# Output projection in two groups of 1024 columns, with the weight sums of the first group formed in DRAM

## Chip, cores and metric

One core of a Trainium2 chip runs the whole kernel. The metric is the device time of one execution in microseconds. All times are of this one core: the median of the runs of the kernel before, and the span of one profiled execution.

## What is computed

One layer of a bidirectional encoder: an RMS norm, one input projection, attention with eight heads over 512 tokens, a recurrent group (convolution and two linear scans), gates, and an output projection that is added to the input. The change touches the last of these alone. Cut to what matters:

```python
def hybrid_layer(x, norm_w, w_in, ..., w_out):
    h = rms_norm(x, norm_w)
    proj = jnp.einsum('bsd,de->bse', h, w_in)
    ...
    mixed = jnp.concatenate([rms_norm(attn_out, attn_norm_w) * jax.nn.silu(g_attn),
                             rms_norm(lru_out, lru_norm_w) * jax.nn.silu(g_lru)], axis=-1)
    return x + jnp.einsum('bse,ed->bsd', mixed, w_out)
```

`x` has 512 rows and 2048 columns, `mixed` 512 by 2048, `w_out` 2048 by 2048, all float32.

## The kernel before

**Numbers.** Each float32 operand of a matmul is split into a rounded high part (a cast on ScalarE, ACT) and the rest (a subtraction on VectorE, DVE). A product is then three matmuls: high by high, high by low, low by high. A weight block therefore costs a DMA, a cast and a subtraction before TensorE (PE) can use it.

**Order.** PE's instructions stand in the order in which the code is written. ACT, DVE, GpSimd (POOL) and SyncE (SP, which issues nearly all DMAs) are ordered by a scheduler that takes ready instructions by priority; loads and splits of weights get a high one. In every engine an instruction that waits holds up all behind it.

**Start.** The first input projection multiplies the first 512 columns of the recurrent input while x arrives: SP loads x in eight chunks (`xload`, L221) beside the weights (`wraw`, L191), PE transposes them (L228), DVE forms sums of squares (L237). `xstats` makes of these `rstd`: a sum on DVE (L270), then two small operations on POOL (`rsqrt_mean`, L254 and L255). `rows` turns `rstd` into a broadcast row `rbc`: four products with the identity on DVE (L263), one matmul on PE (L265), one copy. Every result of a projection is multiplied by `rbc` when it leaves PSUM (`evac_bc`, L364). The splits of the projections' weights are L202 (ACT) and L203 (DVE).

**Middle.** The other projections fill PE while the recurrences and the attention run. POOL computes small norms and scales the softmax weights (L566).

**Output stage.** `outputs` (L704) works in four groups of 512 columns. The 16 row blocks of `w_out` are taken in eight pairs of 256 rows; `mixed` is kept as eight pairs of features in the same way. For the first six pairs a group uses the seven-product form of a 2 by 2 block product (four sums of weight blocks, L670 to L672, and four sums of feature blocks made once, `build`), each product 256 tokens by 256 columns, that is two row tiles of three matmuls with 256 columns (L727). The last two pairs use the plain eight products with 512 columns (L748). The four products that several results share (P1, Q6, Q5, Q7) have PSUM banks of their own and are combined on DVE after the sixth pair (L780 to L787); the others and the plain ones accumulate in the results' banks. At a group's end the residual `xt` is added (L793) and stored through SP (L794). In the last group one row tile is split into two halves of 256 columns so that the last add and store are small.

Of the kernel before, what the change touches and what calls it, by code (L numbers as in the profile page):

```python
# [16 lines left out]
P = 128  # L17
# [38 lines left out]
def hybrid_kernel(  # L56
# [45 lines left out]
    ps = ctx.enter_context(tc.tile_pool(name="ps", bufs=4, space=bass.MemoryType.PSUM))  # L102

# [583 lines left out]
    def four(src, hi, lo):  # L687
        src = halves(src)
        nc.scalar.copy(hi, src)
        nc.vector.tensor_sub(lo, src, f(hi))  # L690

# [3 lines left out]
    def wkept(n):  # L695
        i = turn_of[0] % 3
        turn_of[0] += 1
        pool = pools["out" if i else "fin"]
        return [
            pool.tile([P, 7, H], F32R, tag=f"{t}{i}", bufs=1, name=nm(t))[:, :n]  # L700
            for t in ("wh", "wl")
        ]

    def outputs(work):  # L704

        for c in range(DM // SEQ):
            xt, comb = (
                pools["out"].tile([P, NT, SEQ], F32, tag=t, bufs=1, name=nm(t)) for t in ("xt", "cb")
            )
            cs = slice(c * SEQ, (c + 1) * SEQ)  # L710
            rows_ = [slice(t * P, (t + 1) * P) for t in range(NT)]
            for t in range(NT):
                nc.sync.dma_start(xt[:, t], xf[rows_[t], cs])

            acc = {k: pj().rearrange("p (s e) -> p s e", e=H) for k in (P1, Q6, Q5, Q7)}
            own = [mm() for _ in range(NT)]
            fresh = set(acc) | set(range(NT))

            def mult(k, s, ah, al, a, bh, bl, b_, last):
                ts_ = slice(s * P, (s + 1) * P)  # L720
                if k in acc:
                    dst, bank = acc[k][:, s, :], k
                else:
                    bank = s if k == Q4 else 2 + s
                    dst = own[bank][:, H:] if k in (P2, Q4) else own[bank][:, :H]
                for lh, rh in ((ah, bh), (ah, bl), (al, bh)):
                    nc.tensor.matmul(  # L727
                        dst, lh[:, a, ts_], rh[:, b_, :], start=bank in fresh,
                        stop=last and s == 1 and rh is bh and lh is al, skip_group_check=True,
                    )  # L730
                    fresh.discard(bank)


            end = c == DM // SEQ - 1
            lasts = [pj()[:, :H], own[1][:, H:]] if end else []

            def whole(t, ah, al, bh, bl, last):

                ts_ = slice(t % 2 * P, (t % 2 + 1) * P)
                for half in range(2 if t == 1 and end else 1):  # L740
                    for k in range(2):
                        a, w = 2 * k + t // 2, slice(2 * k, 2 * k + 2)
                        dst = own[t].rearrange("p (j e) -> p j e", e=H)
                        if t == 1 and end:
                            dst, w = lasts[half], 2 * k + half
                        for j, (lh, rh) in enumerate(((ah, bh), (ah, bl), (al, bh))):
                            new = t == 1 and end and half == 0 and k == 0 and j == 0 and not last
                            nc.tensor.matmul(  # L748
                                dst, lh[:, a, ts_], rh[:, w], start=new,
                                stop=last and k == 1 and j == 2, skip_group_check=True,  # L750
                            )

            for i, (r0, A) in enumerate(mixed):
                with tc.high_priority(AHEAD):
                    (raw,) = wraw(w_out, r0, c * SEQ)
                    if i < 6:
                        bh, bl = wkept(7)
                        seven(raw, ALU.add, bh, bl)
                    else:
                        bh, bl = wkept(4)  # L760
                        four(raw, bh, bl)
                if c == 0:
                    next(work, None)
                    A = mixed[i][1]
                ah, al = A
                if i < 6:
                    for k in (P1, Q6, Q5, Q7, P2, Q3, Q4):
                        for s in range(2):
                            mult(k, s, ah, al, k[0], bh, bl, k[1], i == 5 and k in (P1, Q6, Q5, Q7))
                else:  # L770
                    for t in (2, 3, 0, 1):
                        whole(t, ah, al, bh, bl, i == 7)
                if i == 5:
                    with tc.high_priority(AHEAD):

                        def blk(i, j):
                            return comb[:, 2 * i : 2 * i + 2, j * H : (j + 1) * H]

                        v2 = fin_s((P, 2, H))
                        nc.scalar.copy(blk(1, 1), acc[P1])  # L780
                        nc.vector.tensor_sub(v2, acc[Q6], blk(1, 1))
                        nc.vector.tensor_add(blk(1, 0), acc[Q5], v2)
                        nc.vector.tensor_add(blk(0, 0), acc[Q7], blk(1, 0))
                        nc.vector.scalar_tensor_tensor(
                            blk(0, 1), acc[Q7], -1.0, v2, op0=ALU.mult, op1=ALU.subtract
                        )
                        nc.vector.tensor_add(xt, xt, comb)  # L787
            with tc.high_priority(AHEAD):
                parts = [(t, 0, SEQ, own[t]) for t in (2, 3, 0, 1)]
                if end:  # L790
                    parts[3:] = [(1, j * H, (j + 1) * H, lasts[j]) for j in range(2)]
                for t, e0, e1, src in parts:
                    nc.vector.tensor_add(xt[:, t, e0:e1], src, xt[:, t, e0:e1])  # L793
                    nc.sync.dma_start(  # L794
                        of[rows_[t], cs.start + e0 : cs.start + e1], xt[:, t, e0:e1]
                    )
# [60 lines left out]
    lru_consts()  # L857
    fill = proj_feat(C_XR + SEQ, a2)
# [4 lines left out]

    def kv_proj():
        yield from proj_tok(C_K, a3)
# [12 lines left out]
    def q_proj(c0, acc):  # L878
        yield from proj_tok(c0, acc)
        rots.append(norm_rope(evac_tok(acc, ev), G, rq))  # L880
# [15 lines left out]
    def gates():  # L896
        todo = iter(())
        for n, (c0, row) in enumerate(((C_GL, R_LN), (C_GL + SEQ, R_LN + 4), (C_GA, R_AN))):
            acc, wait = [], 0
            for k, _ in enumerate(proj_feat(c0, acc)):  # L900
                if n == 0 and k >= 16 and k % 4 == 0:
# [116 lines left out]
```

## Time and profile before

| | us |
|---|---|
| median of three runs (668.01 to 669.76) | 669.5 |
| span of the profiled execution (first to last instruction) | 668.2 |
| output stage, first to end of last matmul | 500.83 to 664.54 |
| PE busy / DVE busy / ACT busy / POOL busy | 662.1 / 486.2 / 331.5 / 56.8 |
| mean granted TensorE clock | 1.000 |

The page gives the busy time of each engine, the chain of work that ended last, and the costliest groups of instructions with their mean duration. An engine that is busy nearly all the time and makes up the chain sets the time. "Busy" of PE counts overlapping matmuls, so the pace of matmuls is the distance between their starts. DMA shares are of the 16 DMA engines.

The DMA busy share over the span, in 40 slices of 16.7 us, and what was moved:

```profile
DMA  8843252322244311421122211232335364362711
GB/s 286 273 138 95 64 157 71 96 63 70 89 126 127 98 60 36 122 64 54 41 65 64 63 40 56 63 95 66 94 124 187 99 214 129 116 211 88 244 40 63
```

The first two slices, in which x and the first weights arrive, have the highest share of the program.

### The profile page before, as it was taken

The page shows a single profiled execution, that of the slowest core. Times are in us where ns is not written, and L with a number is a line of the kernel's source. Part 1 is how long each engine was busy: PE and PEld are TensorE (multiplying, and loading weights), DVE is VectorE, ACT ScalarE, POOL GpSimd, SP SyncE. Part 2 cuts the span into 40 slices and gives each one's busy share as a digit, 9 for nine tenths or more (in the row PEclk, how much of TensorE's full clock was granted, in tenths as well). Part 3 has the DMA queues.
Part 4 walks back from the last instruction along what each step waited for, and adds up shares of the span by engine and source line. Part 5 has one row for each costly group of instructions (what it writes and reads, how often), then busy time and mean ns, then how long its engine had stood idle before and what let it go on. Part 6 is the DMA issues. An engine that isn't in the chain of part 4 may idle for free.

```text
span 668.2 us, 9513 instructions
## 1 busy us (share of the span) xinstructions
PE 662.1 (99%) x3607; PEld 570.9 (85%) x3607; DVE 486.2 (73%) x819; ACT 331.5 (50%) x581; POOL 56.8 (8%) x77
## 2 busy tenths in 40 slices
PE   8999999999999999999999999999999999999997
PEld 6888888888888888888888888888889999899996
DVE  4879688977687853756955668439979994976944
ACT  3543799489766416445643455335436333332320
POOL 0000000000021302121222112110000000000000
PEclk9999999999999999999999999999999999999999
DMA  8843252322244311421122211232335364362711
GB/s 286 273 138 95 64 157 71 96 63 70 89 126 127 98 60 36 122 64 54 41 65 64 63 40 56 63 95 66 94 124 187 99 214 129 116 211 88 244 40 63
DMA packets 43773, 71.06 MB, mean 106 GB/s; under 512 B 2776, under 2 KB 13136, under 8 KB 43728
## 3 DMA queue, kind: packets, MB, share of 16 engines
q1 hardware_dynamic: 43408, 69.93, 34.2%
q8 instruction: 28, 0.46, 0.3%
q10 hardware_dynamic: 320, 0.53, 0.3%
q14 instruction: 17, 0.14, 0.1%
HBM read 66.25 MB, written 4.19 MB: 105 GB/s over the span
## 4 chain that ended last, share of the span: by engine, by line
PE 99%; DMA 1%; ACTq 0%; DVE 0%; issue 0%
PE pj L143 19%; PE pj L145 19%; PE pj L144 19%; PE pj L727 10%; PE mm L727 8%; PE mm L748 6%; PE mm L145 3%; PE mm L144 3%; PE mm L143 3%; PE mm L573 2%; PE mm L228 1%; PE pj L285 1%; PE mm L521 1%; DMA nw_st<-in_norm_w_dram 1%; PE mm L265 0%; PE mm L641 0%
## 5 line engine op out<-in xcount | busy, mean ns | idle before, releaser
L143 PE MATMUL pj<-x,wh 128*128 128x512 f32 x376 | 149.8, 398 | 0.0
L145 PE MATMUL pj<-x,wl 128*128 128x512 f32 x376 | 146.7, 390 | 0.0
L144 PE MATMUL pj<-x,wh 128*128 128x512 f32 x376 | 146.5, 390 | 0.0
L202 ACT CAST wh<-wr 128x512 fp32r<-128x512 f32 x144 | 86.6, 618 | 75.8 <-PE pj L145 28.8
L203 DVE TENSOR_TENSOR wl<-wr,wh 128x512 fp32r<-128x512 f32 x144 | 100.2, 716 | 30.7 <-ACT wh L202 30.5
L145 PEld LDWEIGHTS pj<-x,wl 128*128 128x128 f32 x376 | 70.6, 188 | 15.2
L144 PEld LDWEIGHTS pj<-x,wh 128*128 128x128 f32 x376 | 70.8, 188 | 13.8 <-issue 0.5
L143 PEld LDWEIGHTS pj<-x,wh 128*128 128x128 f32 x376 | 70.6, 188 | 13.6 <-issue 0.5
L143 PE MATMUL pj<-wh,x 128*128 128x512 f32 x192 | 75.9, 395 | 0.0
L144 PE MATMUL pj<-wl,x 128*128 128x512 f32 x192 | 75.1, 391 | 0.0
L145 PE MATMUL pj<-wh,x 128*128 128x512 f32 x192 | 75.0, 391 | 0.0
L727 PE MATMUL pj<-wh,ml 128*128 128x256 f32 x192 | 54.1, 282 | 0.0
L727 PE MATMUL pj<-wh,mh 128*128 128x256 f32 x192 | 54.0, 281 | 0.0
L727 PE MATMUL pj<-wl,mh 128*128 128x256 f32 x192 | 53.8, 280 | 0.0
L684 ACT CAST wh<-wr 128x768 fp32r<-128x768 f32 x24 | 20.1, 837 | 62.2 <-issue 46.6
L575 ACT CAST b<-mm 128x512 fp32r<-128x512 f32 x32 | 18.8, 586 | 59.8 <-PE mm L573 59.8
L561 DVE TENSOR_REDUCE mx<-mm 128x1 f32<-128x512 f32 x32 | 22.0, 689 | 31.1 <-PE mm L145 30.6
L145 PEld LDWEIGHTS pj<-wh,x 128*128 128x128 f32 x192 | 36.1, 188 | 8.1
L143 PEld LDWEIGHTS pj<-wh,x 128*128 128x128 f32 x192 | 36.0, 188 | 8.0 <-issue 0.2
L144 PEld LDWEIGHTS pj<-wl,x 128*128 128x128 f32 x192 | 36.1, 188 | 7.9 <-issue 0.2
L727 PE MATMUL mm<-wh,ml 128*128 128x256 f32 x144 | 40.5, 282 | 0.0
L727 PE MATMUL mm<-wh,mh 128*128 128x256 f32 x144 | 40.5, 281 | 0.0
(207 smaller groups left out, 1334.0 us busy)
## 6 DMA issues: line engine op xcount, KB each, us to landing
wr<-in_w_in_dram SPq DMA_DIRECT2D x71, 512.0 KB, 3.6
wr<-in_w_out_dram SPq DMA_DIRECT2D x32, 512.0 KB, 4.0
xt<-in_x_dram SPq DMA_DIRECT2D x16, 256.0 KB, 4.4
out_dram<-xt SPq DMA_DIRECT2D x15, 256.0 KB, 3.6
b<-in_x_dram SPq DMA_DIRECT2D x7, 512.0 KB, 7.6
k<-in_lru_wa_dram SPq DMA_DIRECT2D x8, 128.0 KB, 3.8
k<-in_lru_wx_dram SPq DMA_DIRECT2D x8, 128.0 KB, 3.2
wr<-in_w_in_dram ACTq DMA_DIRECT2D x2, 256.0 KB, 4.7
```

Source lines behind the costliest of these rows:

```text
L143: nc.tensor.matmul(acc, lh, rh, start=start, stop=False)
L144: nc.tensor.matmul(acc, lh, rl, start=False, stop=False)
L145: nc.tensor.matmul(acc, ll, rh, start=False, stop=stop)
L202: nc.scalar.copy(hi, raw[:, k, :])
L203: nc.vector.tensor_sub(lo, raw[:, k, :], f(hi))
L228: nc.tensor.transpose(pt[:, t * P : (t + 1) * P], xc[:, t, ks], ident)
L561: nc.vector.tensor_reduce(mx, sc, axis=AX.X, op=ALU.max, negate=True)
L573: nc.tensor.transpose(pt[:, s * P : (s + 1) * P], p[:, s * P : (s + 1) * P], ident)
L575: nc.scalar.copy(pth[:, :, tt], p3)
L684: nc.scalar.copy(hi[:, to], part)
L727: nc.tensor.matmul(dst, lh[:, a, ts_], rh[:, b_, :], start=bank in fresh, stop=last and s == 1 and rh is bh and lh is al, skip_group_check ...
L748: nc.tensor.matmul(dst, lh[:, a, ts_], rh[:, w], start=new, stop=last and k == 1 and j == 2, skip_group_check=True,)
```

## The change

- The output projection has two groups of 1024 columns. All eight pairs use the seven-product form, each product with 512 columns, so that a result of one row tile fills a whole PSUM bank.
- A group goes over the pairs twice: P1, Q6, Q5, Q7 in the first pass, P2, Q3, Q4 in the second (`PASS`). In each pass the first six pairs are taken pair by pair, the last two product by product (`TAIL`), so that banks end one after the other. `done` combines a product with the residual when its bank ends.
- An operand of weights is one block of 128 by 512 (`operand`: cast and subtraction), in nine buffers; `prepare` works eight operands ahead of PE. Raw blocks have six buffers (`load`).
- The sums of weight blocks for the first group are made in DRAM tiles (`tsum`): 16 copies and 16 accumulating DMAs from POOL (`sums_in_dram`), written at intervals into the projections (`paced`, `gates`). For the second group DVE forms them in SBUF (`out_loads`, `kept_c`).
- In the output stage ACT, DVE and SP are also in written order. Stores of the first group, and some of the second, are issued by POOL.
- `residual` loads the residual of a group as four tiles of 128 by 1024. The tiles have four buffers, so the second group's loads wait for the first group's stores.

```diff
+    dp = ctx.enter_context(tc.tile_pool(name="dp", bufs=1, space=bass.MemoryType.DRAM))
...
+    def sums_in_dram():
...
+        def put(c, t, src):
+            nc.gpsimd.dma_start(tsum[c][t], src)
+
+        def add(c, t, src):
+            nc.gpsimd.dma_start(tsum[c][t], src, accum_op=ALU.add)
+
+        for c0 in (0, 2):
+            cs = (c0, c0 + 1)
+            for c in cs:
+                yield put(c, TA, two(c, 0, 1))
+                yield put(c, TB, two(c, 1, 0))
+            for c in cs:
+                yield add(c, TA, two(c, 0, 0))
+                yield add(c, TB, two(c, 0, 0))
+            for c in cs:
+                yield put(c, TC, tsum[c][TA])
+            for c in cs:
+                yield add(c, TC, two(c, 1, 0))
+            for c in cs:
+                yield put(c, TD, tsum[c][TC])
+            for c in cs:
+                yield add(c, TD, two(c, 1, 1))
+
+    def out_loads(g, second, i):
+
+        add = nc.vector.tensor_add
+        if g == 0:
+            t = [tsum[i // 2][k][:, i % 2, :] for k in range(4)]
+            for src in (
+                (blk(i, 1, 1), blk(i, 1, 0), t[TD]) if second else (blk(i, 0, 1), t[TC], t[TA], t[TB])
+            ):
+                yield load(src)
+        elif not second:
+            b12, b11, b21 = load(blk(i, 0, 3)), load(blk(i, 0, 2)), load(blk(i, 1, 2))
+            yield b12
+            add(b12, b12, b11)
+            kept_c[i] = aring.tile([P, SEQ], F32, name=nm("tc"))
+            add(kept_c[i], b12, b21)
+            add(b11, b11, b21)
...
+            elif name == "Q7":
+                v.tensor_add(tmp["c", s], bank[name, s], tmp["c", s])
+                v.tensor_add(tmp["b", s], bank[name, s], tmp["b", s])
+                v.tensor_add(b00, b00, tmp["c", s])
+                v.tensor_sub(b01, b01, tmp["b", s])
+                store(g, s, 0)
...
+        for n, use in enumerate(order_):
+            g, second, k, i = use
+            prepare(n + NW - 1)
+            if n == 0:
+                xts[0] = residual(0)
...
+            if use == (1, 0, 0, 0):
+                xts[1] = residual(1)
...
+    jobs = sums_in_dram()
...
+    def paced(steps, n):
+        for k, step in enumerate(steps):
+            if k % n == n // 2:
+                next(jobs, None)
+            yield step
```

What the scheduler and the written order make of this shows in the built programs. POOL at the start of the program: before, `rstd` follows the constants (`ident`, `ones`, `nhalf`), and next come the norms of K (`rr`).

```order
L151 MEMSET ones 128x128
masks.py:199 ISA
masks.py:199 AFFINE_SELECT ident<-ident 128x128 [waits Pool_49]
L153 MEMSET nhalf 128x48
L254 TENSOR_SCALAR rstd<-xsum 128x4 [waits DVE_49]
L255 TENSOR_TENSOR rstd<-rstd,nhalf 128x4 [waits Pool_49]
```

After, `ts` are the DRAM tiles (four for each of four row groups, 96 to 111); L734 is a copy and L737 an accumulating DMA, each of 512 KB; a wait on a DMASW semaphore is for an earlier of these transfers to have landed.

```order
L734 DMA ts_100<-in_w_out_dram 256x1x512
...
L737 DMA ts_100<-in_w_out_dram 256x1x512 [waits DMASW2_49]
...
L734 DMA ts_102<-ts_100 16x8192 [waits DMASW6_49]
...
L737 DMA ts_102<-in_w_out_dram 256x1x512 [waits DMASW1_49]
...
L734 DMA ts_103<-ts_102 16x8192 [waits DMASW7_49,DMASW4_49]
...
L737 DMA ts_103<-in_w_out_dram 256x1x512 [waits DMASW7_49,DMASW2_49]
L734 DMA ts_109<-in_w_out_dram 256x1x512
...
L737 DMA ts_109<-in_w_out_dram 256x1x512 [waits DMASW3_49]
L255 TENSOR_SCALAR rstd<-xsum 128x4 [waits DVE_49]
L734 DMA ts_106<-ts_104 16x8192 [waits DMASW4_49]
L256 TENSOR_TENSOR rstd<-rstd,nhalf 128x4 [waits Pool_49]
```

Between the constants and `rstd` now stand 24 of the 32 transfers (the rows shown are one chain of them); eight more follow, all ahead of the norms of K.

SP where one group passes into the next: before, the stores (`out_dram<-xt`) and the next residual stand between weights (`wr`) of 512 KB.

```order
L191 DMA wr_5767<-in_w_out_dram 128x2x512 [waits DMAHW6_49,DMAHW3_49,DVE_49]
L794 DMA out_dram<-xt_5124 128x512 [waits DMAHW7_49,DVE_49]
L794 DMA out_dram<-xt_5124 128x512 [waits DVE_49] x3
L191 DMA wr_5821<-in_w_out_dram 128x2x512 [waits DMAHW4_49,DVE_49]
L713 DMA xt_5537<-in_x_dram 128x512 [waits DMAHW2_49,DMAHW7_49,DMAHW1_49,DMAHW0_49]
L713 DMA xt_5537<-in_x_dram 128x512 [waits DMAHW5_49]
```

After, `rw` are raw weight blocks of 256 KB, `xt` the second group's residual tiles of 512 KB; the DMASW semaphores are those of POOL's stores.

```order
L712 DMA rw_5504<-in_w_out_dram 128x512 [waits DMAHW0_49,DVE_49]
L712 DMA rw_5506<-in_w_out_dram 128x512 [waits DMAHW1_49,DVE_49]
L815 DMA xt_5560<-in_x_dram 128x1024 [waits DMASW4_49,DMASW2_49,DVE_49]
L815 DMA xt_5562<-in_x_dram 128x1024 [waits DMASW5_49,DMASW3_49,DVE_49]
L815 DMA xt_5564<-in_x_dram 128x1024 [waits DMASW6_49,DMAHW2_49,DMASW0_49,DVE_49]
L815 DMA xt_5566<-in_x_dram 128x1024 [waits DMASW7_49,DMAHW3_49,DMASW1_49,DVE_49]
L712 DMA rw_5576<-in_w_out_dram 128x512 [waits DMAHW4_49]
```

The weights of the second group's third pair (`rw_5576`) stand behind the four residual loads, which wait for POOL's stores.

DVE where shared products end: before, the combination of a group stands in one piece among the splits of the next group's weights.

```order
L784 SCALAR_TENSOR_TENSOR cb_4678<-pj_4686,s_5049 128x2x256
L685 TENSOR_TENSOR wl_5141<-wr_5138,wh_5140 128x768 [waits Activation_49]
L787 TENSOR_TENSOR xt_4677<-xt_4677,cb_4678 128x2048 [waits DMAHW6_49,DMAHW4_49,DVE_49]
L685 TENSOR_TENSOR wl_5141<-t_1012_5142,wh_5140 128x1024 [waits Activation_49]
L672 TENSOR_TENSOR t_1016_5196<-t_1016_5196,wr_5192 128x256
```

After, at the end of the second group's first pass, `ev` are the partial sums, `ol` the low parts of operands for the second pass, `tc` kept weight sums; `mm` and `pj` are PSUM banks, those of Q6 and Q5, then (`pj_5614`) of Q7.

```order
L851 TENSOR_TENSOR ev_5924<-mm_5590,ev_5898 128x512 [waits PE_49]
L852 TENSOR_TENSOR xt_5566<-xt_5566,ev_5898 128x512 [waits DMASW7_49,DMASW1_49]
L704 TENSOR_TENSOR ol_5932<-rw_5927,oh_5931 128x512 [waits DMAHW0_49,Activation_49]
L704 TENSOR_TENSOR ol_5936<-rw_5929,oh_5935 128x512 [waits DMAHW1_49,Activation_49]
L854 TENSOR_TENSOR ev_5945<-mm_5602,ev_5915 128x512 [waits DVE_49,PE_49]
L855 TENSOR_TENSOR xt_5564<-xt_5564,ev_5945 128x512 [waits DVE_49]
L854 TENSOR_TENSOR ev_5954<-mm_5606,ev_5924 128x512 [waits PE_49]
L855 TENSOR_TENSOR xt_5566<-xt_5566,ev_5954 128x512 [waits DVE_49]
L779 TENSOR_TENSOR tc_5529<-tc_5529,rw_5927 128x512
L704 TENSOR_TENSOR ol_5959<-tc_5529,oh_5958 128x512 [waits Activation_49]
L704 TENSOR_TENSOR ol_5967<-rw_5962,oh_5966 128x512 [waits DMAHW2_49,Activation_49]
L857 TENSOR_TENSOR ev_5945<-pj_5614,ev_5945 128x512 [waits PE_49]
```

With two operations ahead of these and `L858` behind them they are the 15 operations from Q6's end to the two reads of Q7's first bank; two sums of a partial result and the residual now follow each bank, and the splits for the second pass stand between them.

More of the change, by code (lines that the diff above doesn't have):

```diff
@@ L689, in four @@
         nc.scalar.copy(hi, src)
         nc.vector.tensor_sub(lo, src, f(hi))
-    def kept(pool, n=7):
-        return [pool.tile([P, n, H], F32R, tag=t, bufs=1, name=t) for t in (nm("mh"), nm("ml"))]
[L695 to L702, printed above, removed]
-    def outputs(work):
[L706 to L726, printed above, removed]
@@ new lines, in hybrid_kernel, with prepare, residual @@
+    order_ = list(uses())
+    ready, src_of, todo_ = {}, {}, [0]
+    def prepare(upto):
+        while todo_[0] < min(upto, len(order_)):
+            g, second, k, i = use = order_[todo_[0]]
+            todo_[0] += 1
+            if (g, second, i) not in src_of:
+                src_of[g, second, i] = out_loads(g, second, i)
+            ready[use] = operand(next(src_of[g, second, i]))
+    def residual(g):
+        xt = []
+        for t in range(NT):
+            xt.append(pools["out"].tile([P, 2 * SEQ], F32, tag="xt", bufs=NT, name=nm("xt")))
+            nc.sync.dma_start(xt[t], xf[t * P : (t + 1) * P, 2 * g * SEQ : 2 * (g + 1) * SEQ])
+        return xt
@@ L753, in outputs @@
[L753 to L796, printed above, removed]
+                        dst, lh[:, a, ts_], rh[:, es], start=i == 0 and j == 0,
@@ L921, in hybrid_kernel, with build @@
     rows(gbc, r, fin_s((P, NT, P)))
[L924 to L931 removed]
+    def build(i, pair, where):
+        mixed[i][1] = hi, lo = where(7)
+        seven(pair, ALU.subtract, hi, lo)
     for q in range(4):
@@ L950, in later @@
             normed(pair)
+    drain(jobs)
     acc = []
```

171 lines of the change are left out of this document (136 added, 35 removed).

## The prediction

> **What bounds the kernel now.** I read the page's totals first, then the chain that ended last, then that chain piece by piece in the output stage.
>
> ```profile
> span 668.2 us, 9513 instructions
> PE 662.1 (99%) x3607; PEld 570.9 (85%) x3607; DVE 486.2 (73%) x819; ACT 331.5 (50%) x581; POOL 56.8 (8%) x77
> PE 99%; DMA 1%; ACTq 0%; DVE 0%; issue 0%
> ```
>
> TensorE sets the time: the chain of waits is 99% PE. A matmul saved is time saved, and a wait put ahead of one is time lost. The profiled span, 668.2 us, lies 1.3 us below the median of the runs, 669.5; that 1.3 is added at the end. A measurement of this kernel can tell about 0.3%, 2 us, from no change. The records of matmuls overlap, so their pace has to come from the chain:
>
> ```profile
> 500.83 2.88 PE pj L727 x24
> 503.71 2.16 PE mm L727 x18
> ...
> 530.79 11.06 PE mm L748 x48
> 541.86 2.80 PE pj L727 x24
> ...
> 663.81 0.73 PE mm L748 x6
> ```
>
> Between 500.83 and 530.79 stand 6 x 42 = 252 matmuls of 256 columns, 118.9 ns each; 48 of 512 columns take 11.06 us, 230.4 ns each. A column costs nearly the same in both, so width alone brings little.
>
> **Term 1, the matmuls: -8.7 us.** The stage now runs from 500.83 to 664.54, 163.7 us. Afterwards it has 2 groups x 8 pairs x 7 products x 2 row tiles x 3 = 672 matmuls, 24 of them split into halves: 648 x 0.2304 + 48 x 0.1189 = 155.0 us. Ahead of the stage PE's work is the same, and the last add and store keep their form.
>
> **Term 2, the sums in DRAM: +19 us.** The code spreads 32 transfers over the projections, but POOL's built order has 24 of them ahead of rstd (the order rows above), and 18 of these must have landed: 12 copies and 6 adds. What rstd releases, and how late it may be, comes from the timeline and the chain:
>
> ```profile
> 43.87 0.56 POOL L254 TENSOR_SCALAR rstd<-xsum 128x4 f32<-128x4 f32 x1 [42.39 <-DVE xsum L270]
> 45.59 0.88 DVE L263 TENSOR_SCALAR k<-ident,rstd 128x128 f32<-128x128 f32 x4 [1.21 <-POOL rstd L255]
> 48.43 0.69 DVE L203 TENSOR_TENSOR wl<-wr,wh 128x512 fp32r<-128x512 f32 x1 [1.97 <-ACT wh L202]
> 55.62 0.86 PE mm L265 x2
> ```
>
> While L263 waits, every later DVE instruction waits behind it, the weight split at 48.43 first. That split serves the last weight block of the first projection; L265 stands six matmuls (six times about 0.23, 1.4 us) into that block, which therefore starts at 54.2. Going back by one split (0.69), L263 (0.88) and a hand-over (0.1), L263 may start at 52.5; L254 stands 1.7 ahead of it, so 50.9 at the latest. Today it starts at 43.87: **7.0 us of slack**. Beyond it PE loses what POOL loses.
>
> What do 18 transfers of 524,288 bytes take? No row shows a transfer from DRAM to DRAM, nor an add. The nearest rows are the loads, here by window (the last two numbers are the DMA share and GB/s) and by issue (KB each, us to landing):
>
> ```profile
> 0.00:50.90 50.90, 48.47 (x239) 39.94 (x240) 34.22 (x108) 21.97 (x36) 2.51 (x10) 1.00 0.72 229
> 5.00:10.00 5.00, 4.62 (x18) 3.74 (x19) 2.16 (x4) 1.36 (x3) 0.00 (x0) 1.00 1.08 377
> 43.87:55.62 11.75, 11.75 (x54) 9.66 (x53) 8.03 (x33) 3.23 (x6) 1.60 (x2) 1.00 0.37 112
> ...
> 2.29 0.51 SPq L191 DMA_DIRECT2D wr<-in_w_in_dram  x1
> wr<-in_w_in_dram SPq DMA_DIRECT2D x71, 512.0 KB, 3.6
> b<-in_x_dram SPq DMA_DIRECT2D x7, 512.0 KB, 7.6
> ...
> 193.40 0.20 POOL L254 TENSOR_SCALAR rr<-rr 128x2 f32<-128x2 f32 x1 [147.85 <-ACT sh L496]
> ```
>
> With all DMA engines busy (share 1.08) they move 377 GB/s. Up to 50.9 us they are 0.72 busy, so 0.28 x 50.9 = 14.3 us are free. Copies need 6.29 MB / 377 = 16.7 us. An add reads two streams and writes one where a copy reads one and writes one; I take 1.5 copies, between 1 and 2: 3.15 MB x 1.5 / 377 = 12.5 us (8.3 to 16.7). Together 29.2, and 14.9 don't fit (10.7 to 19.1). The free time can't all be used either: the waits form a chain of six (copy ts_100, add, copy to ts_102, add, copy to ts_103, then copy ts_109), and each link of 512 KB has 3.6 - 1.4 = 2.2 us in which it moves nothing; with two or three in flight I charge a third of 13, 4 us. So 19, from 11 to 27. Whether PE meets it at rstd or earlier at x chunks that land late (512 KB beside others: 7.6 instead of 3.6), it is the same missing DMA time. The bounds further out: 0, if transfers cost nothing beside the loads, and 31, if an add costs three copies (25.1 us, 27.5 missing). The last eight transfers hinder nobody: POOL's next work stands at 193.40.
>
> The Trainium skill (DMA: Bandwidth & Descriptors, section Anatomy of one DMA — SWDGE (gpsimd) path) speaks against this term: a transfer from POOL takes about 2.0 us plus its bytes at 436 GB/s. For 524,288 bytes that is an estimate of 3.2 us, six in a chain 19 us, and by it POOL would be at rstd in time and this term 0. The same page (section Issuing engines are not separate DMA queues) says that all queues share 16 engines and interleave, by which the term stands. No run here shows POOL transfers; the shared sum is the stricter of the two.
>
> **Term 3, VectorE in the first group: +0.5 us (0 to 3).** The output stage has PE, ACT and DVE each in the written order. PE takes 6 x 0.2304 = 1.38 us for one operand; DVE works eight operands ahead.
>
> ```profile
> 510.86 1.28 DVE L670 TENSOR_TENSOR t<-wr 128x512 f32<-128x512 f32 x2
> ...
> L202 ACT CAST wh<-wr 128x512 fp32r<-128x512 f32 x144 | 86.6, 618 | 75.8 <-PE pj L145 28.8 <-PE pj L144 21.2 <-issue 19.2
> L671 DVE TENSOR_TENSOR t<-t,wr 128x256 f32<-128x256 f32 x24 | 10.0, 419 | 0.3
> L685 DVE TENSOR_TENSOR ml<-t,mh 128x1024 fp32r<-128x1024 f32 x6 | 7.3, 1210 | 0.0
> L685 DVE TENSOR_TENSOR ml<-hs,mh 128x768 fp32r<-128x768 f32 x4 | 3.8, 943 | 0.0
> ...
> 541.80:582.80 41.00, 41.00 (x303) 38.95 (x302) 30.37 (x43) 13.40 (x15) 0.00 (x0) 1.00 0.47 148
> ```
>
> Two 512-wide operations back to back take 1.28, 0.64 each. Up to the sixth pair's first operand DVE has one projection result, 19 operands, two builds (0.64 + 2 x 0.42 + 0.94 + 1.21 = 3.6) and eight gate operations: 28 x 0.64 + 7.2 = 25.1 us, and PE wants it after 20 x 1.38 = 27.6. The next point, the seventh pair after the third build, is 6.2 later for DVE and 5.5 for PE. It fits by 2 us, less hand-overs between ACT and DVE, hence 0.5. ACT's 0.62 an operand hides behind PE's 1.38. Loads are 7 x 262 KB in 9.7 us, 189 GB/s where before 148 were moved, half of what the engines can.
>
> **Term 4, SyncE held up by the second residual: +3.7 us (1.5 to 8).** In SP's order the four residual loads stand ahead of the third pair's weights, and each waits for the first group's stores from the same tile.
>
> ```profile
> out_dram<-xt SPq DMA_DIRECT2D x15, 256.0 KB, 3.6
> ```
>
> Let T be the end of the first group on PE. The last add ends at T + 0.7. Its store goes through POOL; no row shows one, and I take a store of SP, 3.6 and 0.5 of issue (double that for the upper bound). SP goes on at T + 4.8. Three residual loads and the weights behind them, 1.83 MB, take 4.9 us at 377 GB/s and land 2.2 later, at T + 11.9. Cast and subtraction (0.62 + 0.64) and a hand-over make the operand ready at T + 13.3; PE wants it at T + 8 x 1.38 = 11.0: 2.3 lost. The pair's second operand needs three additions ahead of its own split, and DVE has no lead left, 1.4 more.
>
> **Term 5, VectorE frees a bank late: +2 us (0 to 5).** From there DVE gains 5.53 - 7 x 0.64 = 1.05 us a pair, 4.2 until the last two pairs start on PE (S). Up to the two reads that free Q7's first bank it has 18 splits and additions and the 15 operations of the order rows above, 21.1 us: S + 16.9. The split last product wants that bank after eight operands of the first pass, two and a half of the second and half a tile, S + 10.8 x 1.38 = 14.9.
>
> **Sum.** -8.7 + 19 + 0.5 + 3.7 + 2 = +16.5: span 684.7, time **686.0 us**.
>
> **Rivals.**
> - *POOL reaches rstd in time* (the faster side). Place: POOL's order at the start; it decides at 50.9 us. If each link lands in the 3.6 us of a quiet load, plus 0.5 of issue, six take 25 us and term 2 is 0; quick stores and residual loads also halve term 4: -8.7 + 0.5 + 1.8 + 2 = -4.4, **665 us**. For it: DMA is only 0.37 busy from 43.87 on. Against: the first 30 us are nearly full, and 11 MB need time at any latency. 0.13, a third of it within 0.3%.
> - *Adds are dearer*: three copies each, 31 us at the start, **698 us**, and up to 714 if links land in 7.6 and more while the engines are shared. For it: an add has two reads, and the order makes it wait. Chance 0.20.
> - *Cheaper transfers*: DRAM to DRAM at half the price of a load, 14.6 us, just fits the 14.3; the 4 us of the chain and terms 3 to 5 remain, -8.7 + 4 + 6.2 = +1.5: **671 us**, up to 677. Against: 377 GB/s was reached with the same rows of 2 KB. Chance 0.15.
>
> **How the numbers follow.** The forecast, start between 11 and 27 with terms 3 to 5 in their bounds, holds 0.52: 677 to 697. Faster 0.09, within 0.3% 0.08 (the rest of the first rival, a quarter of the third), slower 0.83. The range from 668 to 714 leaves out a tenth at either end.
>
> **What would show it.** Right: L265 or a weight split on PE waiting at 55 to 80 us, rstd's POOL instruction after 50.9, DMA share near 1 until then; the output stage 155 us of matmuls with one wait a third of the way into the second group's first pass and one at its second pass. Wrong: rstd at 44 to 50 us and PE without a gap, or a stage in which PE never waits.

## The result and the profile after

The changed kernel takes 745.4 us (743.5 to 745.9, median of 4 runs) beside 668.8 for the kernel before (668.0 to 669.8): a ratio of 1.114, 95% interval 1.112 to 1.116. The forecast was 686.0, in a range from 668 to 714, which the result leaves by 31.4 us. Slower was right; the loss is 76.6 us where 16.5 were forecast. The profiled execution has a span of 744.1 us where 668.2 stood.

First the page's totals of the changed kernel: span, engines, the busy tenths of TensorE and its granted clock in 40 slices of 18.6 us, and the shares of the chain that ended last.

```profile
span 744.1 us, 8870 instructions
PE 666.6 (90%) x3091; PEld 546.5 (73%) x3091; DVE 488.8 (66%) x851; ACT 343.4 (46%) x639; POOL 90.3 (12%) x121
PE   7793019999999999999999999999999899959897
PEclk9998558999999999999999999999999999989999
PE 65%; issue 12%; DVE 9%; DMA 8%; POOL 3%; ACT 2%; DVEq 0%; ACTq 0%; SPq 0%; POOLq 0%
```

PE's share of the chain has fallen from 99% to 65%. The tenths show where: a hole in the fourth to sixth slice, and dents in the last nine. What PE waited for is in the view of its waits (us in total, times, longest):

```profile
PE pj L146 <- DVE wl L204: 46.8, 1, 46.8
PE pj L891 <- ACT oh L703: 7.4, 1, 7.4
PE mm L891 <- DVE ol L704: 4.0, 3, 2.8
PE pj L891 <- DVE ev L858: 4.0, 1, 4.0
...
PE pj L891 <- DVE xt L869: 1.5, 1, 1.5
```

One wait of 46.8 us for a weight split is most of the loss. The rows of the output stage (its first and last matmuls), of the gap and of a window in it (us, busy us of PE, PEld, DVE, ACT and POOL, then clock, DMA share, GB/s) place it:

```profile
L891 PE MATMUL mm<-oh,mh x128: 278/394/632, 560.6 to 739.2; 128*128 128x512 f32 x120, 128*128 128x256 f32 x8
739.39 0.37 PE mm L891 x3
109.75 0.79 PE L146 MATMUL pj<-x,wl 128*128 128x512 f32 x1 [46.85 <-DVE wl L204]
80.00:100.00 20.00, 0.00 (x0) 0.00 (x0) 0.00 (x0) 0.00 (x0) 3.90 (x5) 0.50 0.59 105
```

The output stage begins at 560.6 where it began at 500.8: **59.8 us are lost ahead of it**. It then takes 179.2 us (560.6 to 739.8) where it took 163.7: **15.5 more**. The tail adds 0.7. From 80 to 100 us, in the middle of the gap, neither PE nor DVE nor ACT does anything, and the DMA engines are 0.59 busy: whatever is waited for, it is not their bandwidth. POOL's timeline says what it is (start, duration, and in brackets how long POOL had been idle and what ended it):

```profile
1.56 2.20 POOL L734 DMA_DIRECT2D ts<-in_w_out_dram  x3
8.99 0.66 POOL L734 DMA_DIRECT2D ts<-in_w_out_dram  x1 [5.22 <-issue]
14.25 1.11 POOL L737 DMA_DIRECT2D ts<-in_w_out_dram  x1 [4.61 <-issue]
24.08 1.08 POOL L737 DMA_DIRECT2D ts<-in_w_out_dram  x1 [8.72 <-issue]
...
91.99 1.05 POOL L737 DMA_DIRECT2D ts<-in_w_out_dram  x1 [5.24 <-issue]
...
105.18 1.05 POOL L737 DMA_DIRECT2D ts<-in_w_out_dram  x1 [5.63 <-issue]
106.30 0.20 POOL L255 TENSOR_SCALAR rstd<-xsum 128x4 f32<-128x4 f32 x1
L737 POOL DMA_DIRECT2D ts<-in_w_out_dram x16 | 17.0, 1064 | 92.4 <-issue 76.4 <-DMA ts<-ts 16.0
```

The additions (L737) are issued one at a time, 6.3 to 6.7 us apart even in the quiet stretch from 86 us on. There each starts 0.3 us after the one ahead has landed: the one of 91.99 takes 6.2 us to landing, to 98.2, and the next starts at 98.51. In the last row (all 16, four of them behind rstd), 76.4 of the 92.4 us that POOL waits ahead of them are "issue": no wait of the program ends them. The fourth plain copy, which waits for nothing in the program, stands 5.2 us in the same way. So POOL reaches rstd at 106.3 instead of 43.9, and the rest is as the prediction had it: PE loses what POOL loses.

### The profile page after: what moved, and what is told of

It is laid out like the page before. It is cut to its first block, busy times and chain, and to the rows that moved or that the text cites. A ratio compares the mean times of both kernels' runs of the same rounds, so it can differ in the third digit from the quotient of the medians.

```text
span 744.1 us, 8870 instructions
## 1 busy us (share of the span) xinstructions
PE 666.6 (90%) x3091; PEld 546.5 (73%) x3091; DVE 488.8 (66%) x851; ACT 343.4 (46%) x639; POOL 90.3 (12%) x121
## 3 DMA queue, kind: packets, MB, share of 16 engines
q1 hardware_dynamic: 45648, 75.17, 31.6%
q0 software_dynamic: 6720, 19.93, 11.5%
## 4 chain that ended last, share of the span: by engine, by line
PE 65%; issue 12%; DVE 9%; DMA 8%; POOL 3%; ACT 2%; DVEq 0%; ACTq 0%; SPq 0%; POOLq 0%
PE pj L144 16%; PE pj L146 16%; PE pj L145 16%; PE mm L891 3%; DMA rw<-in_w_out_dram 3%; PE mm L146 3%; PE mm L144 3%; PE mm L145 3%; PE pj L891 3%; DVE ol L704 3%; DMA ts<-ts 3%; PE mm L574 2%; POOL ts L737 2%; ACT oh L703 2%; DMA rw<-ts 1%
## 5 line engine op out<-in xcount | busy, mean ns | idle before, releaser
L146 PE MATMUL pj<-x,wl 128*128 128x512 f32 x376 | 148.1, 394 | 46.8 <-DVE wl L204 46.8
L144 PE MATMUL pj<-x,wh 128*128 128x512 f32 x376 | 152.1, 404 | 2.6 <-DVE ev L365 1.4
L145 PE MATMUL pj<-x,wh 128*128 128x512 f32 x376 | 147.9, 393 | 0.4 <-DVE x L232 0.4
L144 PEld LDWEIGHTS pj<-x,wh 128*128 128x128 f32 x376 | 71.5, 190 | 17.7 <-issue 1.6
L145 PEld LDWEIGHTS pj<-x,wh 128*128 128x128 f32 x376 | 71.6, 190 | 15.0 <-issue 0.8
L704 DVE TENSOR_TENSOR ol<-rw,oh 128x512 fp32r<-128x512 f32 x94 | 60.3, 685 | 30.5 <-ACT oh L703 30.4
L703 ACT CAST oh<-rw 128x512 fp32r<-128x512 f32 x94 | 54.2, 618 | 53.5 <-DMA rw<-in_w_out_dram 34.0
L891 PE MATMUL mm<-ol,mh 128*128 128x512 f32 (+1 forms) x128 | 50.7, 396 | 4.1 <-DVE ol L704 4.0
L891 PE MATMUL pj<-oh,mh 128*128 128x512 f32 (+1 forms) x104 | 41.2, 396 | 12.8 <-ACT oh L703 7.4
L891 PE MATMUL mm<-oh,mh 128*128 128x512 f32 (+1 forms) x128 | 50.6, 396 | 0.1
L891 PE MATMUL mm<-oh,ml 128*128 128x512 f32 (+1 forms) x128 | 50.1, 392 | 0.0
```

The costliest lines, as they stand in the source:

```text
L144: nc.tensor.matmul(acc, lh, rh, start=start, stop=False)
L145: nc.tensor.matmul(acc, lh, rl, start=False, stop=False)
L146: nc.tensor.matmul(acc, ll, rh, start=False, stop=stop)
L891: nc.tensor.matmul(dst, lh[:, a, ts_], rh[:, es], start=i == 0 and j == 0, stop=i == 7 and j == 2,)
```

## The experiments

Kernels e1 to e12 have one timed run each beside one of the kernel before (668.1 to 670.0 us), e13 has seven.

**What holds the start.** The first four kernels take the sums away, turn additions into copies, give POOL's transfers more room, and put POOL's work in written order.

```diff
e1:  - t = [tsum[i // 2][k][:, i % 2, :] for k in range(4)]
     + t = [blk(i, 1, 1), blk(i, 1, 0), blk(i, 0, 1), blk(i, 0, 0)]
     - jobs = sums_in_dram()
     + jobs = iter(())
e2:  - nc.gpsimd.dma_start(tsum[c][t], src, accum_op=ALU.add)
     + nc.gpsimd.dma_start(tsum[c][t], src)
e3:  - dynamic_dma_scratch_size=1024
     + dynamic_dma_scratch_size=2048
e4:  - tc.manual_schedule(engines={mybir.EngineType.PE})
     + tc.manual_schedule(engines={mybir.EngineType.PE, mybir.EngineType.Pool})
```

> The changed kernel without any transfer on POOL at the start: the first group loads plain blocks of w_out in the place of the sums, so its products are of other operands (the sums are left out); loads of the same size in the same order, everything else as in the changed kernel. Theory A (POOL, held by the sums ahead of rstd, costs the whole of the 59.7 us that the output stage starts later, and nothing in the stage comes from the sums): the stage starts within 2 us of 500.8, takes 177 to 181, total 684 to 688. Rival B (the start is late for another reason in the change, such as a changed order of loads or weights): the stage starts later than 505. Rival C (reading sums out of DRAM costs the stage something too): the stage is below 175 and the total below 682.

Measured: 684.7 us; the stage starts at 500.7 and takes 178. Theory A holds: without the sums the start is that of before, and the stage's loss remains, with the same three waits (6.4, 4.8 and 3.9 us). Here is rstd on POOL:

```profile
43.89 0.56 POOL L255 TENSOR_SCALAR rstd<-xsum 128x4 f32<-128x4 f32 x1 [42.40 <-DVE xsum L271]
```

> The changed kernel with its 16 additions turned into plain copies of the same blocks to the same places (the additions are left out), same order and same waits. Theory A (an addition isn't issued before the addition ahead of it has landed, 6.6 us each, and that is what holds POOL; copies aren't held so): POOL is at rstd by 50 us, the start loses at most 8 us, total 684 to 695. Rival D (what the prediction said: the DMA engines have too little free time; 24 transfers of 0.52 MB are 33 us at 377 GB/s where 14 are free): rstd at 60 to 75, total 698 to 715. Rival E (any transfer from DRAM to DRAM is slow on POOL): rstd after 90, total above 730.

Measured: 717.6 us. Theory A is out; rival D has rstd right (60 to 75) and the total 2.6 us too low (698 to 715). POOL is through the transfers ahead of rstd at 63.4 us, and yet rstd stands at 73.45: it waits 10.0 us for its input, since the x chunks land late (median 19.7 us from issue to landing, 7.6 before).

```profile
62.77 0.65 POOL L737 DMA_DIRECT2D ts<-in_w_out_dram  x1 [3.56 <-issue]
73.45 0.56 POOL L255 TENSOR_SCALAR rstd<-xsum 128x4 f32<-128x4 f32 x1 [10.02 <-DVE xsum L271]
40.00:60.00 20.00, 13.06 (x54) 10.39 (x54) 8.56 (x23) 6.92 (x12) 5.12 (x8) 0.83 1.00 358
q0 software_dynamic: 3008, 12.58, 49.0%
```

From 40 to 60 us the DMA engines are the bound, as the prediction said of the whole: share 1.00. The last row (POOL's queue up to 73.2 us: packets, MB, share of the engines' time) says 49.0% of 73.2 = 35.9 us for 24 copies, 1.5 us of all 16 engines each.

> The changed kernel with one number changed: the scratch that POOL's transfers write their descriptors into, dynamic_dma_scratch_size, from 1024 to 2048. Theory A1 (POOL waits for room in that scratch: 256 rows of 2 KB read twice and written once fill it, so one addition at a time fits, and the fourth plain copy had to wait too): with twice the room two or three additions are in flight, the fourth copy is issued at 2 us rather than at 9, POOL is at rstd at 60 to 80 us, total 700 to 722. Theory A2 (additions are carried out one after another whatever the room): the additions stay 6.6 us apart, rstd at 104 to 108, total 741 to 748.

Measured: 732.4 us. POOL's timeline with twice the room:

```profile
1.55 2.89 POOL L734 DMA_DIRECT2D ts<-in_w_out_dram  x4
9.38 1.11 POOL L737 DMA_DIRECT2D ts<-in_w_out_dram  x1 [4.95 <-DMA ts<-in_w_out_dram]
12.26 1.08 POOL L737 DMA_DIRECT2D ts<-in_w_out_dram  x1 [1.77 <-DMA ts<-in_w_out_dram]
14.69 1.04 POOL L737 DMA_DIRECT2D ts<-in_w_out_dram  x1 [1.35 <-DMA ts<-in_w_out_dram]
...
69.28 1.05 POOL L737 DMA_DIRECT2D ts<-in_w_out_dram  x1 [4.12 <-issue]
87.46 0.56 POOL L255 TENSOR_SCALAR rstd<-xsum 128x4 f32<-128x4 f32 x1 [17.12 <-DVE xsum L271]
q0 software_dynamic: 4544, 12.58, 61.6%
```

A1's signs are there: four copies at once, three additions within 5.3 us although the first takes 11.5 us to landing, the waits ahead of these ended by landings that the program asks for, and POOL free at 70.3 instead of 106.2. A2 is out. The room still tells: four later additions, the one at 69.28 among them, stand 2.9 to 5.5 us with "issue" as the end of the wait. But the total missed A1's range too: rstd now waits 17.1 us for xsum. POOL's queue took 61.6% of 87.2 = 53.7 us of the engines; with the copies at 1.5 each, an addition is by estimate (53.7 - 12 x 1.5) / 12 = 3.0 us, two copies. Room was the first limit; behind it stands the one that was forecast.

> The changed kernel with POOL's instructions in the order in which they are written, so that rstd comes ahead of all transfers and these stand where the code has them, through the projections and the attention; the same transfers and additions, the result whole. Theory A (the place alone costs the start; between 110 and 540 us POOL has 430 us for 16 additions of 6.6): the stage starts within 3 us of 500.8, total 684 to 689. Rival F (POOL's other work, the rr and r_l pairs and L567, now waits behind additions, up to 7 us each time, and PE meets some of them): the stage starts at 505 to 520, total 690 to 705.

Measured: 694.7 us, rival F: the stage starts at 509.1. POOL's view and PE's one wait there:

```profile
203.63 1.15 POOL L737 DMA_DIRECT2D ts<-in_w_out_dram  x1
225.59 1.05 POOL L737 DMA_DIRECT2D ts<-in_w_out_dram  x1 [5.47 <-issue]
226.71 0.20 POOL L255 TENSOR_SCALAR rr<-rr 128x4 f32<-128x4 f32 x1
247.01 2.07 PE L266 MATMUL mm<-kv,ones 128*128 128x512 f32 x2 [5.71 <-DVE kv L264]
```

Four additions from 203.6 to 226.6 hold up the rr pairs. The next result from POOL that PE waits for, r_l, then comes at 244.1, where it comes at 235.1 in the next kernel (e5). Wherever something waited for stands behind additions on POOL, it pays.

**The place alone, and the stage.** Each kernel of this row adds one edit to the one ahead of it.

```diff
e5 (to e4):   jobs = sums_in_dram()
            + drain(jobs)
e6 (to e5): - if use == (1, 0, 0, 0):
            + if use == (1, 0, 0, 3):
                  xts[1] = residual(1)
e7 (to e6): b11, b00, b01 into the residual: v.tensor_add / v.tensor_sub -> nc.gpsimd
e8 (to e7): - add = nc.vector.tensor_add
            + add = nc.gpsimd.tensor_add
e9 (to e6): - if n == 0:
            + if use == (0, 0, 0, 3):
                  xts[0] = residual(0)
e10 (to e9): - add(kept_c[i], kept_c[i], b22)
             + nc.gpsimd.tensor_add(kept_c[i], kept_c[i], b22)
e11 (to e10): e7's edit
```

> The changed kernel with POOL's instructions in written order and all 32 transfers written right behind rstd, where POOL's next other work (rr) stands 148 us later; the result whole. Theory A (the place ahead of rstd is the whole cost of the sums; 16 additions of 6.6 us and 16 copies fit into 148 us): the stage starts within 2 us of 500.8, total 683 to 688, like the run without sums. Rival G (beside these transfers the weights of the second projection land late): PE waits for weights or weight splits between 45 and 180 us, total 690 to 705.

Measured: 686.7 us, the stage from 499.7. Theory A holds: the same 32 transfers, the additions still about 7 us apart (63.88, 71.00, 77.86), are all issued by 188 us, ahead of POOL's next other work at 192.5, and PE has no gap from 40 to 192 us.

> As the run before it in this list, and the second group's four residual loads are issued three operands of pair 1 later, at the fourth pair-0 operand of the group, that is behind the weights of two or three more pairs in SP's order. Term 4 of the prediction (SP is held by the first group's last stores) says: the wait of 7.4 us at ACT's cast goes, and the 6.8 us at half clock around it, total 673 to 677. Rival H (the raw buffers or VectorE would have held these operands anyway): the wait stays over 4 us, total above 680.

(The place that this text names is wrong: the loads stand at the first operand of the group's fourth pair, 12 operands later.) Measured: 672.5 us, 14.3 less, a little beyond what was expected; ACT's wait is gone. What it had been is in the changed kernel's rows: SP's stall at the residual loads, POOL's stores, and the chain through them.

```profile
648.99 9.01 SPq L815 DMA_DIRECT2D xt<-in_x_dram  x4
650.66 0.54 POOL L822 DMA_DIRECT2D out_dram<-xt  x1 [3.38 <-DVE xt L869]
651.37 6.15 DMA out_dram<-xt
658.04 6.28 DMA rw<-in_w_out_dram
665.09 0.80 PE L891 MATMUL pj<-oh,mh 128*128 128x512 f32 x1 [7.37 <-ACT oh L703]
```

The store is issued, lands 6.15 us later, and only then do the weights start, to land after another 6.28. In the last row a matmul takes 0.80 where the median is 0.39: behind this pause PE runs near half clock for some us (granted clock 0.59 from 665.1 to 669).

> As the late residual, and the three additions into the residual that read no PSUM (into b11, b00 and b01, four of each kind) are done by GpSimd instead of VectorE. Term 5 (VectorE frees Q7's first bank late) says: VectorE is 12 x 0.68 = 8.2 us less busy, half of it in the second group, and reaches the read that frees the bank 2.5 us earlier or more; the wait of 3.9 us for L858 falls below 1.5 us, total 3 to 6 us less than the late residual. Rival I (GpSimd's slower additions, 1.3 us, now hold a temporary that VectorE or ACT wants next): the wait stays or grows, total the same or more.

Measured: 671.9 us, 0.5 less, which single runs can't tell from nothing; the wait for L858 stays at 2.6. The edit didn't lighten VectorE either. Twelve additions of 0.68 us are gone from it, but from 499 to 662 us it is busy for 134.6 us where it was for 131.8 in e6; the subtractions of L704, 60.3 us in e6, have grown:

```profile
L704 DVE TENSOR_TENSOR ol<-rw,oh 128x512 fp32r<-128x512 f32 x94 | 66.4, 751 | 17.3 <-ACT oh L703 17.2
```

So this run says nothing for or against term 5's reason.

> As the run before it in this list, and the four sums of each pair of the second group are formed by GpSimd too: VectorE is 32 x 0.69 = 22 us less busy in the second group, GpSimd 32 x 1.3 = 42 us busier of 80. If VectorE is what PE still waits for in the second group: no wait over 1 us there, total 662 to 668, level with or below the kernel before. Rival J (an operand made from a sum now comes 3 x 1.3 us after its last load, and GpSimd is in the chain): PE waits at operands of the second group, total above 672.

Measured: 684.8 us, 12.9 more, in rival J's range: PE waits 3.5 us for L869, 7.9 for operands, 2.5 for L858. L704 has grown to 71.7 us here, so J's later operands and VectorE's longer instructions aren't told apart.

> The kernel with the transfers behind rstd and the second residual late, and now the first group's four residual loads (2.1 MB) too stand behind the weights of its first pairs in SP's order, at the fourth pair. Theory K (the waits of 0.84 and 2.82 us early in the stage, which the prediction put at 0.5, come from these loads: they went ahead of the second pair's weights, one of which landed 7.6 us after its issue and left VectorE idle for 6.0 us): both waits go, with the 3.4 us at half clock, total 4 to 6 us less than with the second residual late alone (672.5): 666.5 to 668.5. Rival L (VectorE's own work, the builds and gates, is too much there, as term 3 feared): a wait of 2 us or more stays at 530 to 534, total 670 or more.

Measured: 669.7 us, 2.8 less. The two waits fall from 0.84 and 2.82 to 0.19 and 0.58, as theory K says, but the total misses K's range (666.5 to 668.5): the wait for L858 grows from 2.6 to 3.2 and, unlike that of 2.6, has matmuls at half clock behind it.

> As the run before it in this list, and of the second group's four sums per pair the last one (for the second pass, 0.69 us on VectorE) is formed by GpSimd. Theory M (term 5: VectorE comes 2.6 us late to the reads that free Q7's banks, because three or four of these sums stand ahead of them): the wait for L858 falls by 2 us or goes, total 1.5 to 3 us less than the run before. Rival N (what comes late there is an operand, not VectorE's time): same within 1 us, or more, since GpSimd's addition is slower.

Measured: 665.8 us beside 669.8 for the kernel before, 3.8 less than e9, more than theory M's 1.5 to 3. The largest waits left in the stage:

```profile
PE mm L891 <- DVE ol L704: 1.1, 2, 0.6
PE pj L891 <- DVE ev L858: 0.7, 1, 0.7
```

> As the run before it in this list, with the three additions into the residual on GpSimd as well. Alone these were worth 0.5 us; if VectorE is still what PE waits for at the end of the second group's first pass, 0.5 to 2 us less than the run before, otherwise the same within 1 us.

Measured: 669.8 us, 4 more than e10's single run and 2.3 more than that kernel's median in e13 below, neither case. The rows of GpSimd and VectorE in one stretch of it:

```profile
616.90 3.33 POOL L852 TENSOR_TENSOR xt<-xt,ev 128x512 f32<-128x512 f32 x2 [1.28 <-ACT ev L849]
620.20 1.74 POOL L779 TENSOR_TENSOR tc<-tc,rw 128x512 f32<-128x512 f32 x1
614.38 8.11 DVE L704 TENSOR_TENSOR ol<-rw,oh 128x512 fp32r<-128x512 f32 x6
```

Six subtractions that take 3.7 us in the changed kernel (its row at 561.37, below) take 8.11 while GpSimd adds. GpSimd's additions do not run beside VectorE's, they push them back, which fits e7 and e8. How much of the 4 us this is stays open. The wait for L858 is 2.5 us in e11 and in e13, yet in e11 the matmuls behind it take 0.63 us from 631.4 to 635.7, and in e13 the usual 0.39 to 0.40: a pause of this length is followed by half clock in one run and not in another, and that alone is some 2 us (ten matmuls 0.43 apart instead of 0.23).

**Rows or bytes.** The last kernel on the start keeps the bytes of each addition and cuts its rows to a quarter.

```diff
e12: - nc.gpsimd.dma_start(tsum[c][t], src, accum_op=ALU.add)
     + nc.gpsimd.dma_start(rows8(tsum[c][t]), flat[:, : 4 * SEQ], accum_op=ALU.add)
     + flat = dp.tile([P // 2, 4 * SEQ + 16], F32, tag="flat", bufs=1, name="flat")
     + nc.gpsimd.dma_start(flat[:, : 4 * SEQ], w_in[: P // 2, : 4 * SEQ])
```

> The changed kernel, scratch at 1024 as there, with each of the 16 additions reading one and the same DRAM block of 64 rows of 8 KB (so the sums are others; one more copy fills that block) in the place of 256 rows of 2 KB: the same 0.52 MB per addition, a quarter of the rows. Theory A1 (the room is used up by rows): additions no longer wait for one another, POOL is through the transfers ahead of rstd by 75 us, and what is left is the transfers' share of the engines: total 700 to 735. Theory A3 (the room is used up by bytes, or an addition always waits for the one ahead): additions stay 6 us or more apart, rstd at 95 to 110, total 735 to 750.

Measured: 734.0 us, at the upper end of A1's range. With the scratch at 1024 as in the changed kernel, the additions ahead of rstd (L740 here; L737 is the copy) come in two bursts, 2.4 to 3.8 us apart, while they take a median of 10.6 to landing. They wait only for landings that the program asks for, and POOL is through at 44.6:

```profile
13.57 0.80 POOL L740 DMA_DIRECT2D ts<-flat  x1 [1.51 <-DMA ts<-in_w_out_dram]
...
44.05 0.50 POOL L737 DMA_DIRECT2D ts<-ts  x1 [1.54 <-DMA ts<-flat]
72.06 0.56 POOL L255 TENSOR_SCALAR rstd<-xsum 128x4 f32<-128x4 f32 x1 [27.51 <-DVE xsum L271]
```

So rows fill the room, not bytes (A1; the built order differs from the changed kernel's: six additions now stand ahead of rstd). The gain is spent again: rstd waits 27.5 us for x chunks, and between 80 and 100 us PE is busy 7.8 us of 20 beside the remaining transfers.

**Is that all?** e10's kernel again, timed.

> The kernel of the run e10 again (transfers behind rstd, both residuals late, one sum on GpSimd), timed. If the prediction's term 1 holds (8.7 us fewer matmuls) and the waits found so far are all that stood against it (2.4 us of them are left in the profile of that run, and 1.5 to 2 us more in matmuls that come a little slower than 0.2304), it is 4 to 5 us faster than the kernel before: ratio 0.992 to 0.995. If its one run of 665.8 was a fortunate one, the ratio is within 0.3% of 1.

Measured: 667.5 us (7 runs) beside 669.2 (11 runs), ratio 0.9973, interval 0.9962 to 0.9985. It is faster than the kernel before by 0.3%, less than expected, and e10's 665.8 was fortunate: the lowest run here is 666.8. In this profile the wait for L858 is 2.5 us again, with 1.2 for L869.

```profile
PE pj L891 <- DVE ev L858: 2.5, 1, 2.5
```

The stage takes 161.3 us (500.3 to 661.6) where it took 163.7 before.

## Why the prediction was right and where it failed

- **What bounds the kernel** was right, and so was the link from POOL to PE. PE's last matmul ahead of the gap ends at 62.9, where the prediction had 54.2 without late x chunks, 8.7 later. Its last moment for rstd, 50.9, moves to 59.6 with that, and 106.3 - 59.6 = 46.7 is the gap that PE shows. Gap and late x chunks are 55.5 of the 59.8 us; the rest has the matmuls at half clock behind the gap in it.
- **Term 1** (-8.7): the pace held. Five blocks of twelve 512-column matmuls follow in 13.9 us of the chain, 0.2315 each where 0.2304 was taken. The 155 us were never seen alone: the shortest stage, e10's, takes 159.2 us, and less its 2.4 us of waits 156.8, so some 1.8 us of the 8.7 did not come.
- **Term 2** (+19) is the step that failed; it measured 59.8. It added up the transfers as a share of bandwidth, with 4 us for a chain of six waits. What decided was POOL's own issue, which the sum put at nothing: with the scratch of 1024 one addition of 256 rows is under way at a time, and POOL doesn't get past the next one until the last has landed. Twelve additions, not six, stand ahead of rstd, 6.3 to 11.6 us apart: that is 91 of the 105 us (14.25 to 105.18). The rival with dearer links named this side, but with six links, so its 714 was too low. e3 and e12 show that the room and the rows in it make the wait; e5 shows that the same 32 transfers cost nothing where nothing waits behind them.
- The bandwidth sum itself was too kind as well, though the changed kernel never comes to it. An addition takes the engines two copies (e3), the upper end that was given. All 24 transfers issued ahead of rstd compete with the x chunks, not the 18 that must have landed. By the prediction's own sum e3 gives 53.7 - 14.3 free + 4 = 43.4 us, and its stage starts 45.8 late (546.6 for 500.8); e2 gives 25.6, and its stage starts 31.6 late (532.4).
- The rule of **the Trainium skill** that was weighed there (DMA: Bandwidth & Descriptors, section Anatomy of one DMA — SWDGE (gpsimd) path), by which the estimate was 3.2 us for such a transfer, isn't what the runs show: 6.3 us and more from one addition to the next in a quiet stretch, and medians to landing of 7.3 us for the transfers from w_out and 7.1 for those from ts. The other rule (same page, section Issuing engines are not separate DMA queues) agrees with e2, where the x chunks on SP's queue land late beside POOL's transfers and xsum comes 29.6 us later (73.2 for 43.6).
- **Term 3** (+0.5): 3.7 us of waits, at 578 and 593 in the changed kernel. VectorE's work was counted rightly, but not that the first residual's four loads, 2.1 MB, go ahead of the second pair's weights. VectorE's timeline, a load of the chain and PE's two waits:

```profile
561.37 3.69 DVE L704 TENSOR_TENSOR ol<-rw,oh 128x512 fp32r<-128x512 f32 x6
571.11 2.09 DVE L704 TENSOR_TENSOR ol<-rw,oh 128x512 fp32r<-128x512 f32 x3 [6.05 <-ACT oh L703]
563.33 7.76 DMA rw<-ts
578.66 0.51 PE L891 MATMUL mm<-ol,mh 128*128 128x512 f32 x1 [0.85 <-DVE ol L704]
592.90 0.56 PE L891 MATMUL mm<-ol,mh 128*128 128x512 f32 x1 [2.82 <-DVE ol L704]
```

  The load lands 7.76 us after its issue, and VectorE, counted as busy throughout, is idle for 6.05. In e9 this idle time is 1.48.
- **Term 4** (+3.7): the mechanism was right, the size wrong: 14.3 us by e6 (one run each side). With T = 649.0, the first group's end on PE (1.5 us ahead of 650.5), SP goes on at T + 9.0 instead of T + 4.8: the last add ends at 651.0, not T + 0.7, and the last store lands after 6.15 instead of 3.6. The weights land at T + 15.3 instead of T + 11.9. And PE is out of operands at 657.7, T + 8.7 with that 1.5 us wait in it, instead of T + 11.0: five operands were ready, not eight. The half clock behind the pause, and the wait for L858, which shrinks in e6 from 4.0 to 2.6, are in the 14.3 too, and no run takes them apart.
- **Term 5** (+2): the wait came where forecast, L858, 4.0 us. e10 points to VectorE's sums ahead of it (3.2 in e9 to 0.7), but e13, the same kernel, shows 2.5 again. How much of it is VectorE's own work, and how much its collisions with GpSimd, stays open.
- **No rival** was right on its own. "Cheaper transfers" was wrong by its premise; "POOL reaches rstd in time" is what e5 makes true, and gives 686.7, not 665, because the stage's terms were too small.
- **What was to show it**: the split on PE waiting at 55 to 80 us (62.9), rstd after 50.9 and the two waits of the second group came. A DMA share near 1 until rstd did not: 0.59 from 80 to 100 us is the line that told bandwidth from issue.

## What to carry to other kernels

Price a queue by how many of its transfers can be under way, not only by its bytes: one instruction that the engine can't get past holds everything behind it in order, and here many rows of 2 KB used up the room for descriptors where a quarter as many of 8 KB did not (e12). Read the built order of every engine whose order is left to a scheduler: 32 transfers written across 500 us stood ahead of the one small instruction on which the whole start waits, and moving them behind it was worth 58.7 us. And where a load stands in the order ahead of one that is needed sooner, count its bytes as delay of the other, at a stage's start above all.

## What the runs showed of the hardware

- An accumulating transfer of 0.52 MB from DRAM to DRAM takes about 6.5 us of POOL's order on a quiet core and, by the estimate of e3, 3.0 us of the 16 engines; a plain copy takes 1.5 of these. Additions overlap when the scratch is doubled (e3) or the rows are a quarter as many (e12). The fourth plain copy of 256 rows had to wait at 1024 and not at 2048.
- Held back one at a time, fewer transfers compete with the loads of x. POOL's queue took 22.6 us of the engines (42.9% of 52.7) before xsum in the changed kernel and made it 9.1 us late, 35.9 and 29.6 in e2. So with more room POOL is through sooner and x comes later.
- In the gap PE's granted clock falls to half, 0.50 from 80 to 100 us, and it stays there for some 5 us behind it: 0.51 from 109.75 to 115.5, with matmuls of 0.63 to 0.80 us. Pauses of 2.8 us (592.9 in the changed kernel) and of 3.2 us (e9) are followed by half clock too, those of 2.6 us in e6 and e7 are not, and those of 2.5 us are in e11 and not in e13. The Trainium skill (TensorE: Matmul & The Clock Gate, Part 1: The HAM clock gate) says that a gate sets the clock to half or to full by how busy PE has been of late; the gap's rows agree.
- GpSimd's fp32 additions hold up VectorE's two-operand instructions: 8.11 us for six that take 3.7 alone, and 66.4 us for 94 that take 60.3 (e7, e6). The Trainium skill (SBUF — State Buffer, section Who interferes with whom) states that these two contend for a shared port pair; the row agrees.
